# A hybrid RWKV-7 / RG-LRU layer whose engine programs are ordered by another timing model

## The chip, the cores and the metric

The kernel runs on one core of one Trainium2 chip. Times are device microseconds (us) from the first to the last instruction's work of one execution, as the run reports them; a kernel's time is the median of its runs. The core has five instruction streams that matter here: PE (matrix products, with its weight loads shown apart as PEld), DVE, ACT and POOL (element-wise work), and SP, which issues most of the DMA transfers. Each stream executes its own program strictly in the order in which it stands, and waits for the others through semaphores.

## What is computed

One layer of a diffusion backbone on 128 context tokens and 1024 latent tokens, 1024 wide. Cut to what matters:

```python
h = rmsnorm(x, ln1_g) * (1.0 + sc1) + sh1            # modulation from silu(c) @ w_mod
proj = h @ w_in                                       # r, k, v, xw, xa, xg, xb, gb
r, k, v, xw, xa, xg, xb, gb = jnp.split(proj, SPLITS, axis=-1)
ya, s_fin = rwkv7_mix(r, k, v, xw, xa, xg, s0, ...)   # 8 heads x 64, two directions
yb, h_fin = rglru_mix(xb, gb, h0, ...)                # 8 blocks x 64, two directions
x = x + g1 * (jnp.concatenate([ya, yb], axis=-1) @ w_out)
h = rmsnorm(x, ln2_g) * (1.0 + sc2) + sh2
u = dwconv(h @ w_up, ffn_conv_w, ffn_conv_b, CONV_F_LEFT, grid)
ua, ub = jnp.split(u, 2, axis=-1)
x = x + g2 * ((jax.nn.gelu(ua) * ub) @ w_down)        # then a last rmsnorm
```

`rwkv7_mix` is a recurrence over the tokens with a 64x64 state per head; the RG-LRU is a linear recurrence per channel. Outputs are the two normalised token arrays and the final context states.

## The kernel before, in words

**Precision.** Most products are made of three: an operand is split into a rounded part and a rest (`round_hi` L103, `rest_lo` L110), and `mm3` (L94) multiplies high by high, high by low and low by high. `mm` (L91) is the one place that issues a product, so that all of them carry line L92.

**Stretches.** The program goes through the following in order of time; where one ends and the next begins, they overlap.

- *Start and modulation*, to about 92 us: the inputs and a part of `w_mod` are loaded, tokens are normalised and transposed.
- *Projection*, 92 to 460 us: `proj` (L722) makes a tile of 128 columns of `h @ w_in` in three spans of 384 tokens, each a group of 24 products into one of two PSUM banks (`mm`), which ACT copies out. Beside it run, as generators that are stepped along (`beside`, L983): `unit_keys` (L539), which takes the norm of the keys through `cols2` (L474: a product into bank `uk`, an ACT copy `row`, three transposes back into `uk`, a DVE copy); `stage_ab` with `products` (L628, tile `dg`) and `bonus` (L650: two POOL operations on `kd`, then a product `ab<-kd,rkc`); and `inverse` (L488, tile `iv`), a long chain of DVE operations with a few products at its end.
- *Two lanes*, 460 to 720 us: the recurrence is worked through in hops of 64 tokens by `chain` (L1100). One hop is `prep` (L1079: product `pa<-kxa,BK`, a DVE mask `G`, a POOL scaling of `BK`, transposes, an ACT copy `Kt`) and then a serial sequence: products into `ya` with the state, copies `R` out of it, products `ca<-R,TTp`, copies `VS`, products `ca<-VS,Kt` and `ya<-VS,G`, and the addition into the next state. Lane a makes 32 hops one after the other, lane b 24. The last letter of a tile is its lane: `ya`, `ca`, `pa` are lane a's. Beside them stands the rest of the projection with the RG-LRU (`lru_gates` L863, tile `lg`; `lru_scan` L884).
- *Four lanes*, 720 to about 960 us: lanes c and d (8 hops each, tiles `yc`, `cc`, `pc` and so on) join; `post` (L1277, tile `po`) finishes outputs of the lanes; `mod_rest` (L1335, tile `md`) loads the rest of `w_mod` and multiplies; `wout_lru` (L1413, tile `wo`) makes the RG-LRU half of the output projection. Here all lanes' `p` and `c` tiles share two PSUM banks (`two`, L1442).
- *Output projection of the other half and second norm*, to about 1090 us (`second_norm` L1476); *up projection*, 1090 to 1546 us; *down projection*, 1570 to 1825 us.

**What sets the order.** The Python program emits all instructions in one sequence. Where several generators run beside each other, counts written out by hand share them out, for the two lanes and the rest of the projection, and then for the four lanes:

```python
run_all((take(lane_a, LA), LA), (take(lane_b, LB), LB), (rest_of_projection(), 12 + (54 - 6 * len(EARLY)) * 4 // PK))  # L1250
run_all((lane_a, 98 - LA), (lane_b, 98 - LB), (lane_c, 26), (lane_d, 26), (posts(90), 90),                          # L1445
        (seq(mod_rest(16, 24), beside_all((mod_rest(24, 48), 30), (wout_lru(), 48))), FL))
```

With LA = 74 and LB = 52, 24 hops of lane a and some 17 of lane b are emitted beside the projection's rest. The emitted sequence is not the engines' order yet: when the `TileContext` (L1856) is closed, a scheduler walks through it with a model of the time that each instruction takes, and puts on each engine's program the earliest emitted instruction that the model has ready. The change touches only the function `kernel` at the end, where the context is made.

## Time and profile before

| | |
|---|---|
| median of 3 runs | 1857.11 us (1849.83, 1857.11, 1857.19) |
| the profiled execution's own time | 1849.17 us |
| its span in the profile | 1847.5 us |
| PE busy, weight loads busy | 1716.4 us (93%), 1442.9 us (78%) |
| DVE, ACT, POOL busy | 1272.2, 865.5, 721.8 us |
| mean granted clock of TensorE | 0.954 of 2.4 GHz |

The profile is of one execution. Its page gives busy times by engine and by fortieth of the span; answers of the trace give the same by any stretch, the waits of an engine with what ended them, and groups of instructions with their mean duration and the idle time before them. A wait is charged to the instruction that came last. The granted clock is 1.00 where TensorE had 2.4 GHz all the time, and falls towards 0.5 with the share of time at 1.2 GHz.

### The profile page before, as it was taken

What the parts mean: (1) busy time and instruction counts of PE and PEld (TensorE: products, weight loads), DVE (VectorE), ACT (ScalarE), POOL (GpSimd) and SP (SyncE); (2) the same over time, 40 slices, a digit from 0 to 9 for tenths busy, and PEclk for the clock granted to TensorE, in tenths of its full rate; (3) what the DMA queues carried; (4) which work ended last, traced back from release to release, by engine and by line L of the source; (5) the groups of instructions that cost most, each with busy time, mean ns of one, the idle gap of its engine ahead of it and who ended that gap; (6) DMA issues with size and microseconds to landing.
All of it is one profiled execution on the core that took longest, in us unless ns stands there. A gap on an engine that the chain in (4) does not pass through costs nothing.

```text
span 1847.5 us, 35759 instructions
## 1 busy us (share of the span) xinstructions
PE 1716.4 (93%) x13341; PEld 1442.9 (78%) x13341; DVE 1272.2 (69%) x2633; ACT 865.5 (47%) x1787; POOL 721.8 (39%) x742
## 2 busy tenths in 40 slices
PE   5998898888999989899988789999999998999996
PEld 4776676678777778456656689999999998888885
DVE  5458967797477664476788877676767667576764
ACT  6466655643666756333335844444444443121211
POOL 1022423322355344131121166666666663434340
PEclk8898979889999999899999899999999999999998
DMA  9254544443443434867775222222222225558571
GB/s 300 63 163 155 174 139 135 147 147 118 145 122 97 131 104 146 257 194 231 232 254 189 82 64 86 78 72 72 74 79 75 77 73 171 184 159 262 173 252 57
DMA packets 268428, 264.92 MB, mean 143 GB/s; under 512 B 21173, under 2 KB 218448, under 8 KB 268256
## 3 DMA queue, kind: packets, MB, share of 16 engines
q1 hardware_dynamic: 252496, 245.97, 42.1%
q10 hardware_dynamic: 15472, 16.54, 2.7%
q8 instruction: 105, 1.72, 0.4%
q14 instruction: 67, 0.55, 0.1%
q0 software_dynamic: 288, 0.14, 0.0%
HBM read 188.00 MB, written 74.58 MB: 142 GB/s over the span
## 4 chain that ended last, share of the span: by engine, by line
PE 66%; DVE 9%; ACT 3%; DMA 3%; issue 3%; POOL 3%; SPq 0%; ACTq 0%; POOLq 0%; DVEq 0%
PE acc L92 14%; PE x L92 7%; PE y L92 7%; PE z L92 7%; PE mm L92 7%; PE v L92 3%; PE wo L92 3%; PE ya L92 2%; PE lg L92 2%; PE md L92 2%; PE pa L92 2%; PE ca L92 1%; DVE X L501 1%; PE yb L92 1%; DVE gt L499 1%
## 5 line engine op out<-in xcount | busy, mean ns | idle before, releaser
L92 PE MATMUL mm<-h_hi,winp 128*128 128x384 f32 x1056 | 304.4, 358 | 4.9 <-DVE vr L808 3.2
L92 PEld LDWEIGHTS mm<-h_hi,winp 128*128 128x128 f32 x1056 | 198.7, 196 | 26.4 <-issue 14.9
L92 PE MATMUL mm<-h_lo,winp 128*128 128x384 f32 x528 | 187.7, 356 | 3.0 <-DVE h_lo L112 3.0
L112 POOL TENSOR_TENSOR wl<-raw,wh 128x512 fp32r<-128x512 f32 x110 | 155.1, 1412 | 69.7 <-ACT wh L106 69.4
L106 ACT ACTIVATE wh<-raw 128x512 fp32r<-128x512 f32 x110 | 69.5, 633 | 148.3 <-PE z L92 81.0
L92 PE MATMUL x<-f_hi,wh 128*128 128x256 f32 (+1 forms) x352 | 105.8, 301 | 8.9 <-ACT q L1652 5.3
L92 PEld LDWEIGHTS mm<-h_lo,winp 128*128 128x128 f32 x528 | 103.7, 197 | 9.6 <-DVE h_lo L112 4.5
L1090 POOL TENSOR_TENSOR BK<-BK,pc 128x256 f32<-128x256 f32 x72 | 47.8, 664 | 150.5 <-PE pa L92 58.8
L92 PE MATMUL x<-f_lo,wh 128*128 128x256 f32 (+1 forms) x352 | 105.5, 300 | 0.2 <-DVE f_lo L112 0.2
L92 PE MATMUL y<-t_hi,wh 128*128 128x320 f32 (+1 forms) x352 | 104.9, 298 | 0.7 <-DVE q L1657 0.7
L92 PE MATMUL x<-f_hi,wl 128*128 128x256 f32 (+1 forms) x352 | 105.3, 299 | 0.0
L92 PE MATMUL y<-t_lo,wh 128*128 128x320 f32 (+1 forms) x352 | 104.7, 297 | 0.0
L92 PE MATMUL y<-t_hi,wl 128*128 128x320 f32 (+1 forms) x352 | 104.6, 297 | 0.0
L112 POOL TENSOR_TENSOR wl<-S,wh 128x512 fp32r<-128x512 f32 x44 | 57.7, 1311 | 105.6 <-ACT wh L106 105.6
L92 PE MATMUL acc<-f_hi 128*128 128x512 f32 x330 | 91.0, 397 | 3.2 <-ACT zf L1760 3.2
L108 POOL TENSOR_SCALAR t_hi<-raw 128x512 fp32r<-128x512 f32 x66 | 52.9, 804 | 81.6 <-PE acc L92 35.4
L1619 DVE SCALAR_TENSOR_TENSOR zf<-C,fcw,zf 128x567 f32<-128x567 f32 x66 | 63.5, 962 | 23.3 <-ACT zf L1617 23.3
L92 PEld LDWEIGHTS acc<-f_hi 128*128 128x128 f32 x330 | 63.1, 192 | 16.9 <-ACT zf L1760 3.7
L92 PEld LDWEIGHTS x<-f_hi,wh 128*128 128x128 f32 x352 | 67.9, 193 | 9.9 <-ACT q L1652 5.8
L112 DVE TENSOR_TENSOR t_hi<-raw,t_hi 128x512 fp32r<-128x512 f32 x66 | 48.1, 735 | 37.0 <-POOL t_hi L108 37.0
L1617 ACT ACTIVATE zf<-C,colB,fcw 128x576 f32<-128x576 f32 x66 | 57.3, 868 | 28.1 <-DVE C L1689 15.7
L600 POOL TENSOR_TENSOR kd<-kd,rk 128x512 f32<-128x512 f32 (+1 forms) x24 | 32.2, 1342 | 97.0 <-ACT kd L598 96.8
(516 smaller groups left out, 5211.1 us busy)
## 6 DMA issues: line engine op xcount, KB each, us to landing
raw<-in_w_down SPq DMA_DIRECT2D x132, 256.0 KB, 3.1
raw<-in_w_up SPq DMA_DIRECT2D x88, 256.0 KB, 3.0
wmod<-in_w_mod SPq DMA_DIRECT2D x68, 256.0 KB, 4.2
act_d<-zf SPq DMA_DIRECT2D x44, 288.0 KB, 2.2
src<-act_d SPq DMA_DIRECT2D x66, 192.0 KB, 3.8
win<-in_w_in SPq DMA_DIRECT2D x44, 256.0 KB, 3.9
KR<-kb_d SPq DMA_DIRECT2D x36, 256.0 KB, 3.2
VS<-v_d SPq DMA_DIRECT2D x36, 256.0 KB, 3.2
```

The costliest lines, as they stand in the source:

```text
L92: PE.matmul(out, lhsT, rhs, start=start, stop=stop, skip_group_check=True)
L106: A.activation(hi, src, AF.Copy)
L108: eng.tensor_scalar(hi, src, 1.0, 0.0, op0=OP.mult, op1=OP.add)
L112: eng.tensor_tensor(lo, src, hi.bitcast(F32), op=OP.subtract)
L499: V.tensor_tensor(tv, X[:, q + 1:32, q:q + 1].to_broadcast([128, m, q]), X[:, q:q + 1, 0:q].to_broadcast([128, m, q]), op=OP.mult)
L501: V.tensor_tensor(X[:, q + 1:32, 0:q], X[:, q + 1:32, 0:q], tv, op=OP.add)
L600: G.tensor_tensor(self.kd, self.kd, self.k, op=OP.mult)
L1090: G.tensor_tensor(bk, bk, pc_f[q.f][:, :, x:x + 1].to_broadcast([128, 2, 128]), op=OP.mult)
L1617: A.activation(u, src, AF.Identity, scale=fcw[:, 1, m:m + 1], bias=colb("ffn_conv_b", m))
L1619: V.scalar_tensor_tensor(dv[:, :, 1:64], sv[:, :, 0:63], fcw[:, 0, m:m + 1], dv[:, :, 1:64], op0=OP.mult, op1=OP.add)
```

## The change

The scheduler is told to order the engines' programs by the timing of a timeline simulator in place of a core simulator's. The emitted sequence, the tiles, the arithmetic and the DMA transfers stay.

```diff
-    with _tile.TileContext(nc) as tc:
+    with _tile.TileContext(nc, schedule_with_timeline_sim=True) as tc:
         tile_hybrid_step(tc, aps, *outs)
```

Matched by their names, all 10533 products and transposes of PE, 2633 instructions of DVE, 742 of POOL and 989 transfers of SP are the same in both programs, in another order. ACT's loads of function tables, which the build puts in where the function changes, go from 29 to 33. From the up projection to the end PE's order is the same, but for the beginning of the up projection and that of the down projection. Ahead of that it differs throughout. Three places follow; the rows are an engine's instructions in the order of its program (line, operation, output and inputs, output's shape, how often in a row).

PE in the projection, before the change: the last `dg` products of a group, and the `bonus` product `ab<-kd,rkc`, which needs two POOL operations on `kd`; `mm` is a group of the projection.

```order
L92 MATMUL dg<-kr,bk 32x32 x2
L92 MATMUL mm<-h_lo,winp 128x384
L92 MATMUL mm<-h_hi,winp 128x384 x2
L92 MATMUL mm<-h_lo,winp 128x384
L92 MATMUL mm<-h_hi,winp 128x384 x2
L92 MATMUL mm<-h_lo,winp 128x384
L92 MATMUL mm<-h_hi,winp 128x384
L92 MATMUL ab<-kd,rkc 2x512
```

The same product on PE with the change, where the `dg` rows stand 29 rows further up.

```order
L92 MATMUL mm<-h_hi,winp 128x384 x2
L92 MATMUL mm<-h_lo,winp 128x384
L92 MATMUL mm<-h_hi,winp 128x384
L92 MATMUL iv<-T_2008,off 32x32 x32
L92 MATMUL ab<-kd,rkc 2x512
```

Between the last `dg` and `ab` there were 8 products of the projection; now there are 40, and 32 of the inverse. Of the twelve such products in the program, five have moved away from `dg` like this, and seven stand closer to it than before.

PE in the projection, before: the second and third step of the key norms of one tile (`uk<-sq,hsel`, then the transposes of ACT's copy `row` of its result).

```order
L92 MATMUL mm<-h_lo,winp 128x384
L92 MATMUL uk<-sq,hsel 2x384
L92 MATMUL mm<-h_hi,winp 128x384 x2
L92 MATMUL mm<-h_lo,winp 128x384
L92 MATMUL mm<-h_hi,winp 128x384
L484 MATMUL uk<-ident,row 128x2 x3
L92 MATMUL mm<-h_hi,winp 128x384
```

The same on PE with the change.

```order
L92 MATMUL iv<-TT,a_2254 32x32 x32
L484 MATMUL uk<-ident,row 128x2 x3
L92 MATMUL uk<-sq,hsel 2x384
L484 MATMUL uk<-ident,row 128x2 x3
L92 MATMUL mm<-h_hi,winp 128x384
```

Four products of the projection stood between a product into `uk` and the transposes of its copy; now none does, in this place and in others like it.

PE near the end of the four lanes, before: a part of one round in which lanes a, c and d make a hop each.

```order
L92 MATMUL cc<-R,TTp 64x64 x4
L92 MATMUL pc<-kxc,BK 128x256 x2
L92 MATMUL cd<-R,TTp 64x64 x4
L92 MATMUL wo<-woh,ybh 128x512
L92 MATMUL wo<-wol,ybh 128x512
L92 MATMUL wo<-woh,ybl 128x512
L92 MATMUL pd<-kxd,BK 128x256 x2
L92 MATMUL wo<-woh,ybh 128x512
L92 MATMUL wo<-wol,ybh 128x512
L92 MATMUL wo<-woh,ybl 128x512
L92 MATMUL md<-wmod,silx 32x512 x4
L92 MATMUL ca<-VS,Kt 64x64 x4
```

The same part of a round with the change.

```order
L92 MATMUL cc<-R,TTp 64x64 x4
L92 MATMUL yc<-VS,G 64x64
L92 MATMUL cd<-R,TTp 64x64 x4
L92 MATMUL yc<-VS,G 64x64 x3
L92 MATMUL pc<-kxc,BK 128x256 x2
L92 MATMUL yd<-VS,G 64x64
L1094 MATMUL pa<-ident,BK 128x128 x2
L92 MATMUL yd<-VS,G 64x64 x3
L1094 MATMUL pc<-ident,BK 128x128 x2
L92 MATMUL pd<-kxd,BK 128x256 x2
L1094 MATMUL pd<-ident,BK 128x128 x2
L92 MATMUL ca<-VS,Kt 64x64 x4
```

The products of `wo` and `md` have gone from the last five rounds: the last `wo` stands ahead of lane a's 28th hop, where before it stood behind its 32nd. The projection's rest moved up likewise: its last product stands ahead of lane a's 16th hop, where before it stood just ahead of the 25th, and lane a's hops 18 to 25 now stand nearly by themselves, with products of `md`, the first of `wo`, and the first hop of lane d.

## Rows read from the trace of the kernel before

**Rows 1.** The page: the span, and the engines' busy time with its share.

```profile
span 1847.5 us, 35759 instructions
...
PE 1716.4 (93%) x13341; PEld 1442.9 (78%) x13341; DVE 1272.2 (69%) x2633; ACT 865.5 (47%) x1787; POOL 721.8 (39%) x742
```

**Rows 2.** By stretch: length, then each engine's busy time, clock, DMA share, GB/s.

```profile
92.00:460.00 368.00, 334.53 (x3677) 265.47 (x3677) 281.46 (x598) 210.43 (x475) 107.94 (x147) 0.91 0.47 147
460.00:720.00 260.00, 249.65 (x2258) 200.23 (x2257) 164.99 (x334) 173.20 (x352) 118.31 (x122) 0.97 0.39 117
720.00:800.00 80.00, 66.05 (x476) 41.74 (x476) 33.61 (x97) 32.61 (x81) 19.81 (x31) 0.90 0.65 216
800.00:930.00 130.00, 129.23 (x1058) 86.94 (x1058) 98.13 (x289) 49.00 (x139) 25.82 (x38) 1.00 0.74 236
930.00:1090.00 160.00, 131.05 (x787) 105.29 (x786) 130.58 (x298) 86.84 (x195) 44.10 (x35) 0.90 0.47 153
1090.00:1546.00 456.00, 456.00 (x3418) 455.70 (x3418) 322.71 (x555) 203.67 (x329) 293.82 (x225) 1.00 0.25 79
...
1570.00:1825.00 255.00, 255.00 (x1114) 210.84 (x1115) 160.23 (x260) 46.24 (x98) 100.21 (x120) 0.99 0.60 189
```

**Rows 3.** PE's waits, 92 to 460 us: us in total, times, longest.

```profile
PE ab L92 <- POOL kd L652: 9.0, 5, 3.1
...
PE mm L92 <- DVE vr L808: 3.2, 2, 2.2
...
PE ab L92 <- POOL P L606: 2.2, 1, 2.2
```

**Rows 4.** Groups on POOL, whole span: count, then busy us, mean ns of one.

```profile
L652 POOL TENSOR_TENSOR kd<-kd,rk 128x512 f32<-128x512 f32 (+1 forms) x12 | 15.0, 1251 | 0.7
```

**Rows 5.** PE's waits, 720 to 800 us.

```profile
PE pc L92 <- DMA BK<-kb_d: 6.8, 1, 6.8
PE pa L1094 <- DVE S0b L1185: 1.8, 1, 1.8
...
PE cc L92 <- ACT R L1075: 0.8, 1, 0.8
...
PE cc L92 <- ACT VS L1075: 0.5, 1, 0.5
PE cc L92 <- ACT Kt L1095: 0.5, 1, 0.5
```

**Rows 6.** PE's waits, 460 to 720 us.

```profile
PE ca L92 <- DVE R L1077: 5.7, 3, 4.9
```

**Rows 7.** Groups on ACT, whole span: table loads of one line.

```profile
L901 ACT ACT_TABLE_LOAD x5 | 6.4, 1283 | 0.1
```

**Rows 8.** PE in order of time: start, us, and two of lane a's hops beginning.

```profile
486.93 0.61 PE L92 MATMUL ya<-S1a,KR 128*128 128x128 f32 x4
...
493.27 0.61 PE L92 MATMUL ya<-S0a,KR 128*128 128x128 f32 x4
```

**Rows 9.** PE's waits, 800 to 930 us, all of them.

```profile
PE pc L92 <- DVE S0a L1185: 0.4, 1, 0.4
PE wo L92 <- DVE wol L112: 0.3, 1, 0.3
```

**Rows 10.** Groups on PE, 903.3 to 925.8 us, one round of hops.

```profile
L92 PE MATMUL wo<-woh,ybl 128*128 128x512 f32 x13 | 5.4, 414 | 0.0
L92 PE MATMUL wo<-woh,ybh 128*128 128x512 f32 x12 | 5.1, 429 | 0.0
L92 PE MATMUL wo<-wol,ybh 128*128 128x512 f32 x12 | 4.7, 394 | 0.0
L92 PE MATMUL md<-wmod,silx 128*32 128x512 f32 x8 | 2.1, 604 | 0.0
```

**Rows 11.** PE's waits, 930 to 1090 us.

```profile
PE mm L92 <- ACT rv L128: 4.8, 1, 4.8
PE mm L92 <- DVE tm L1408: 4.0, 5, 1.6
```

## The prediction

> **What bounds the kernel now.** I read the busy times first, then the stretches, then PE's waits in each stretch. PE is busy for 93% of the span [rows 1], but the stretches differ [rows 2]. The up projection keeps PE busy for 456.00 of 456 us and the down projection for 255.00 of 255, both at a clock of 0.99 or 1.00. PE's order there is unchanged but for the beginnings, so these 711 us can't get shorter by an order, and with their start fed as before they don't get longer. What the change can touch lies between 92 and 1090 us. PE is idle there for 368 − 334.5 = 33.5 us in the projection, 10.4 in the two lanes, 14 in the first 80 us of the four lanes, 0.8 in the next 130, and 29 up to 1090: 87.7 us in all. Two things are to be seen in the waits. Where PE waits long (2 to 7 us at a time), its program holds a product too early for an input that comes late from POOL, DVE or a DMA [rows 3, 5]. And where independent products stand between a lane's steps, PE hardly waits at all: 0.7 us in 130 [rows 9].
>
> **The change, part by part.** All instructions stay, so the work on every engine stays, apart from four more table loads on ACT. Only waits change, and the clock with them. I count in the two orders how many products stand between a product that needs a copy and the product that the copy was made from.
>
> *Projection.* `ab<-kd` waits for POOL five times, 9.0 us in all, and once more for 2.2 us [rows 3]. One POOL operation on `kd` takes 1.25 us, and two follow each other [rows 4]. In the change, five of the twelve `ab` have 7.8 to 9.6 us of products ahead of them since the last `dg`, where they had 1.7 to 5.9 us before, and four of them waited for over 2 us each. The longest wait was 3.1 us, and these five gain 3.4 to 8 us of cover, so I take 10 of these 11.2 us as gone, and the 3.2 us on `vr` too, whose cover grows likewise: −13. On the other side, the `uk` steps and others like them have lost their cover: I count 27 places in this stretch (3 before) at which less than 0.4 us of products stands between a product and one that needs ACT's or DVE's copy of its result. What such a place costs is seen at the start of the four lanes, where PE waited 0.8, 0.5 and 0.5 us for copies with nothing between [rows 5]. 27 × 0.5 = +13.5. Sum: 0, with ends of −13 (all new places hidden behind other waits) and +13.
>
> *Two lanes.* 5.7 us of waits for `R` [rows 6], most of it one wait of 4.9 us whose cover doesn't grow; I take −2 for the others, and +2 for five new uncovered places. ACT switches between exponential and square root more often, since the two square roots of an RG-LRU block no longer stand side by side: six more table loads here (and fewer elsewhere) at 1.28 us [rows 7]. ACT is busy for 173 of 260 us [rows 2], so I cost them at nothing; if ACT were in a lane's way there, it would be 6 × 1.28 = 7.7 us. Sum: 0, from −5 to +8.
>
> *Start of the four lanes.* PE waited 6.8 us for the first `BK` from DRAM, then for single handovers, 10.4 us in the five rows shown [rows 5]. With the change the projection's rest is through earlier, its memory is free earlier, and these loads run while lane a makes eight hops nearly alone. Those hops cost in turn: a hop takes 493.27 − 486.93 = 6.3 us where nothing holds it up [rows 8], so eight take 51 us. I sum the start-to-start times of the products that now stand in this piece to some 49 us. So PE has work for nearly all of it, and what is lost are handovers: 12 uncovered ones, 12 × 0.55 = +6.5, against −10.4. Sum −4, from −11 to +8; the upper end is one more late transfer of 6.8 us, since PE's program holds `md` products between lane a's steps, and a late `wmod` would hold up lane a, which is queued behind it.
>
> *End of the four lanes.* This is the term that decides. Before, a round of one hop of lanes a, c and d took 22.5 us, of which 15.2 us were products of `wo` and 3.0 or less of `md` [rows 10]; they filled every step, and the stretch ran at clock 1.00 with 0.7 us of waits [rows 2, 9]. With the change no `wo` and no `md` is left for the last five rounds, and the lanes go in step, share two PSUM banks, and wait for the same copies. I count 32 places with less than 0.4 us of cover, where there were none. At 0.55 us (between the 0.5 and 0.8 us of [rows 5]) that is +17.6. The lanes' own products in these rounds come to some 43 us; at the clock of 0.90 that the stretches with waits show, against 1.00 [rows 2], they would take 4.8 us more, of which I take half. Sum +20. It can be 0, if the three lanes cover each other as lanes a and b do around 490 us [rows 8]; at 0.8 us each it is 32 × 0.8 + 4.8 = +30.
>
> *Up to 1090 us.* The first product of the next stretch waited 4.8 us and five others 4.0 us [rows 11]. Their cover grows by 0.6 to 1 us in the change; −4, from −6 to 0. Start, up and down projection: 0. The few DMA issues that change places on SP there have PE's unbroken run in front of them; without that cover one late transfer is again 6.8 us.
>
> Sum: 0 + 0 − 4 + 20 − 4 = **+12 us** on the profiled execution's 1849.2 us. That execution is at the lower of two levels, 7.9 us under the median; the runs shown lie at 1849.8 and at 1857.1 to 1857.2. I set the 12 us on the middle of the levels, 1853, and predict **1865 us**: slower, by 0.65%. About 0.5%, or 9 us, is what a measurement of this kernel can tell from no change.
>
> **The rivals.**
>
> *Gains and losses cancel.* The lanes cover each other at the end for the larger part, and the end costs 6 us in place of 20. Then the sum is −2, and the time 1851. For it speaks the stretch around 490 us, where two lanes alone made hops at 6.3 us; against it, that there each lane had banks of its own, and the order held the lanes out of step. It decides at about 0.2 us per uncovered place.
>
> *Faster: the waits for late inputs were the real loss.* The order by the new timing puts nearly every product that waited before further behind its producer. If those longer distances hold, and the uncovered places in the projection fall into time at which PE would have waited for PSUM copies anyway, then the projection gives −13, the start of the four lanes −11, up to 1090 us −6, and the end costs 10: −20, which is 1833. For it: each wait of 2 us or more in [rows 3] but for the inverse's gets more cover. Against it: 27 places there stand bare where 3 did. The point is whether a bare place in the projection costs less than 0.2 us.
>
> *The weight loads were the bound.* In the 470 us of the lanes (460 to 930 us) PE's products are busy for 444.9 us, its weight loads for only 328.9 [rows 2]. If products that only look busy leave room, a better order can pack the lanes' small products closer, and a quarter of these 116 us would be −29: 1824. Against it: in the part with 0.7 us of waits the clock is 1.00 and DVE is at 98 of 130 us, and nothing there suggests that PE stood idle. The Trainium skill (Perfetto Trace Analysis, Identifying the Most-Contended Engine) says that the busy share of matmuls misjudges the headroom, and that the weight loads' share is the measure; by it these stretches are at 70%, not at 95%, and this rival is the forecast. The trace agrees in the up projection, where both are at 100%, and leaves it open in the lanes.
>
> That the change does nothing is excluded: the orders differ.
>
> **How the numbers follow.** The forecast, slower by over 0.5%, has a chance of 0.45; its own range, by the ends of its largest term, is 1858 to 1885. Cancelling has 0.31, the late inputs 0.19, the weight loads 0.05. So faster is 0.24, the same 0.31, slower 0.45. The range for eight times in ten leaves out the weight loads and the far ends: from 1836, a little above the second rival, to 1888, which is the upper level of 1857 with the end's +30.
>
> **What would show it.** Right: in the changed profile PE's waits for `kd` and `vr` are under 3 us together; the waits for `BK` from DRAM at the start of the four lanes are gone; the last five rounds of hops take 14 to 16 us each, at a clock under 1.00, with PE waiting for `R`, `VS`, `Kt` and `G` some 15 to 25 us in all; the up and down projections take 456 and 255 us as before. Wrong: those five rounds take 10 to 11 us each, or the projection is shorter by over 10 us or longer by as much, or PE waits for `wmod` amid lane a's hops.

## The result and the profile after

The changed kernel takes 1919.86 us (median of 4 runs, 1910.67 to 1930.05) against 1853.47 us (4 runs, 1847.04 to 1857.19): a ratio of 1.0363, 95% interval 1.0286 to 1.0441. It is slower, as forecast, but by over five times as much: 66 us where 12 were forecast, and outside the range. The changed kernel's runs lie at two levels, two near 1911 and two near 1929 us, and the profiled execution is the slowest of the four, 1930.05 us with a span of 1928.1: against the 1847.5 us of [rows 1] it is 80.6 us longer, some 14 us more than the medians differ by.

The page after: the span, and the engines' busy time.

```profile
span 1928.1 us, 35880 instructions
...
PE 1757.1 (91%) x13341; PEld 1489.1 (77%) x13341; DVE 1289.2 (67%) x2633; ACT 860.5 (45%) x1791; POOL 728.2 (38%) x742
```

DVE, ACT and POOL are as busy as in [rows 1] to within 17 us. PE is busy 41 us longer with the same products, at a mean granted clock of 0.929 where it had 0.954. By stretch, with the columns of [rows 2]; the rows after the first begin at the 2851st and the 4351st product of PE's program, and the last ends at the 5251st (the first row begins earlier than the table's projection, as in [rows 2], at 85 us):

```profile
85.00:485.30 400.30, 346.49 (x3690) 284.06 (x3689) 276.49 (x586) 207.49 (x479) 106.98 (x142) 0.85 0.42 132
485.30:823.10 337.80, 307.49 (x2386) 237.68 (x2388) 188.20 (x400) 194.41 (x382) 130.34 (x144) 0.88 0.48 151
823.10:1028.60 205.50, 188.84 (x1500) 129.85 (x1500) 132.11 (x355) 69.92 (x199) 41.91 (x59) 0.96 0.57 180
```

The same stretches of the kernel before, from product to product (the first from 92 us):

```profile
92.00:465.30 373.30, 339.44 (x3694) 268.73 (x3693) 284.35 (x602) 213.68 (x482) 109.34 (x150) 0.91 0.47 148
465.30:757.50 292.20, 272.28 (x2383) 215.37 (x2385) 175.54 (x371) 185.32 (x379) 124.81 (x132) 0.96 0.42 130
757.50:944.50 187.00, 182.25 (x1517) 120.58 (x1516) 129.59 (x376) 70.03 (x197) 39.59 (x58) 0.99 0.72 231
```

Where the 80.6 us came from, in us. "At equal work" corrects for the products that one program has done ahead of a seam and the other not yet (4.4 us at most, by their durations before). "Lost to the clock" is the stretch times what its granted clock lacks to 1.00. The first row begins with PE's first product, 2.7 us into the span; in the last one, idle time and clock are counted up to PE's last product.

| stretch | before | after | difference | at equal work | PE idle, before to after | lost to the clock |
|---|---|---|---|---|---|---|
| start, to the 451st product | 110.8 | 105.8 | −5.0 | −4.4 | 21.0 to 21.4 | 10.2 to 6.8 |
| projection | 351.8 | 376.8 | +25.0 | +26.1 | 33.9 to 51.5 | 34.1 to 59.7 |
| two lanes, lane a's solo hops with them | 292.2 | 337.8 | +45.6 | +39.5 | 19.9 to 30.3 | 11.9 to 39.3 |
| four lanes | 187.0 | 205.6 | +18.6 | +18.8 | 4.8 to 16.7 | 1.7 to 8.5 |
| up to the up projection (5860th) | 145.7 | 147.7 | +2.0 | +6.2 | 28.9 to 31.6 | 16.7 to 16.1 |
| up projection | 459.2 | 459.6 | +0.4 | +0.4 | 0 to 0 | 0.3 to 1.0 |
| down projection and end | 298.0 | 292.2 | −5.8 | −5.8 | 5.2 to 1.3 | 3.4 to 0.0 |

PE's waits in the projection after, 88 to 485 us, which answer to [rows 3]:

```profile
PE ab L484 <- ACT row L480: 10.4, 5, 4.4
PE ab L92 <- ACT b L589: 7.0, 4, 2.6
PE iv L92 <- DVE T L506: 6.7, 4, 2.9
PE dg L92 <- DVE bk L622: 4.2, 5, 1.6
PE uk L484 <- ACT row L480: 4.1, 6, 1.0
...
PE ab L92 <- POOL kd L652: 2.0, 2, 1.2
```

The waits for `kd` went from 9.0 to 2.0 us, and the one for `vr` is gone. In their place PE waits for `row` and `b` from ACT and for `T` and `bk` from DVE, small steps on both.

PE's waits in the two lanes after, 485 to 823 us, the longest ones, which answer to [rows 5, 6]:

```profile
PE ya L92 <- ACT VS L1075: 5.1, 5, 2.4
PE cb L92 <- DVE VS L1077: 4.1, 2, 3.6
PE ya L92 <- DVE S0a L1185: 3.9, 1, 3.9
PE ca L92 <- DVE VS L1077: 3.0, 2, 2.6
PE pa L92 <- DMA KR<-kb_d: 2.8, 1, 2.8
PE cb L92 <- ACT R L1075: 2.7, 2, 2.0
```

The 6.8 us for `BK` from DRAM [rows 5] are gone; one wait of 2.8 us for `KR` from DRAM is new. Otherwise the lanes' own copies and state updates are late, by 2 to 4 us at a time, on DVE as on ACT.

What ACT does in that stretch shows how copies come to be late. ACT in order of time, after:

```profile
509.76 0.27 ACT L1075 ACTIVATE R<-ya 64x128 f32<-64x128 f32 x1
510.06 1.27 ACT L1065 ACTIVATE kxa<-KR 64x512 f32<-64x512 f32 x2
511.36 1.35 ACT L896 ACTIVATE th<-th,lc 128x1152 f32<-128x1152 f32 x1
512.73 0.38 ACT L1095 ACTIVATE Kt<-pa 128x256 f32<-128x256 f32 x1
513.01 1.34 ACT L894 ACTIVATE tz<-th,lc 128x1152 f32<-128x1152 f32 x1
514.36 1.28 ACT L901 ACT_TABLE_LOAD   x1
515.66 1.16 ACT L901 ACTIVATE a<-a 128x1152 f32<-128x1152 f32 x1
516.84 1.28 ACT L896 ACT_TABLE_LOAD   x1
518.13 1.35 ACT L896 ACTIVATE th<-th,lc 128x1152 f32<-128x1152 f32 x1
519.51 1.28 ACT L901 ACT_TABLE_LOAD   x1
520.80 1.17 ACT L901 ACTIVATE a<-a 128x1152 f32<-128x1152 f32 x1
521.99 0.27 ACT L1075 ACTIVATE R<-yb 64x128 f32<-64x128 f32 x1
```

The same gate steps of the RG-LRU before, the middle of the group:

```profile
507.95 1.34 ACT L896 ACTIVATE th<-th,lc 128x1152 f32<-128x1152 f32 x1
509.41 0.27 ACT L1075 ACTIVATE VS<-cb 64x128 f32<-64x128 f32 x1
510.86 0.27 ACT L1075 ACTIVATE R<-ya 64x128 f32<-64x128 f32 x1 [1.18 <-PE ya L92]
511.03 1.34 ACT L894 ACTIVATE tz<-th,lc 128x1152 f32<-128x1152 f32 x1
512.73 0.27 ACT L1075 ACTIVATE VS<-ca 64x128 f32<-64x128 f32 x1 [0.36 <-PE ca L92]
512.91 1.34 ACT L896 ACTIVATE th<-th,lc 128x1152 f32<-128x1152 f32 x1
```

Before, copies `R` and `VS` of the lanes stand between the gate steps shown. After, no `R` and no `VS` runs on ACT from 510.0 to 522.0 us, while five gate steps and three table loads go through nearly in one piece; the last product into `yb` ends at 516.5 us, so the `R<-yb` at 521.99 starts 5.5 us late. There are four such groups in the stretch. Added up over the records of the two lanes, from the moment a copy's input and its target were free to its start, the copies `R` and `VS` on ACT (88 before, 82 after between these seams) wait 69 us instead of 31, and the `Kt` 34 instead of 17. DVE hangs on the same copies. `R` and `VS` are each made in two halves, one by ACT and one by DVE, and in all 82 pairs of either trace DVE's half starts only after ACT's has ended. DVE's waits for that, 485 to 823 us after:

```profile
DVE VS L1077 <- ACT VS L1075: 32.6, 22, 3.9
DVE R L1077 <- ACT R L1075: 20.3, 18, 4.0
```

These 52.9 us were 21.5 before. So a wait that is put down to DVE's half can go back to ACT's. And in the chain of waits (the work that ended last, followed back), the pieces on ACT between 485 and 823 us add up to 56 us; between 465 and 757 us before they were 17. Those on PE are 216 and 212. That is what the experiments start from.

### The profile page after: what moved, and what is told of

Its sections match the earlier page's. It is cut to its first block, busy times and chain, and to the rows that moved or that the text cites. A ratio compares the mean times of both kernels' runs of the same rounds, so it can differ in the third digit from the quotient of the medians.

```text
span 1928.1 us, 35880 instructions
## 1 busy us (share of the span) xinstructions
PE 1757.1 (91%) x13341; PEld 1489.1 (77%) x13341; DVE 1289.2 (67%) x2633; ACT 860.5 (45%) x1791; POOL 728.2 (38%) x742
## 4 chain that ended last, share of the span: by engine, by line
PE 64%; DVE 7%; ACT 6%; DMA 3%; issue 3%; POOL 2%; SPq 1%; ACTq 0%; DVEq 0%; POOLq 0%
PE acc L92 14%; PE mm L92 8%; PE x L92 7%; PE y L92 7%; PE z L92 7%; PE v L92 3%; PE ya L92 2%; PE wo L92 2%; PE lg L92 2%; PE md L92 2%; PE pa L92 2%; PE yb L92 1%; PE ca L92 1%; PE pb L92 1%; ACT xt L1486 1%
## 5 line engine op out<-in xcount | busy, mean ns | idle before, releaser
L92 PEld LDWEIGHTS mm<-h_hi,winp 128*128 128x128 f32 x1056 | 206.5, 203 | 17.6 <-issue 6.8
L112 POOL TENSOR_TENSOR wl<-raw,wh 128x512 fp32r<-128x512 f32 x110 | 149.6, 1361 | 134.8 <-ACT wh L106 134.8
L92 PEld LDWEIGHTS mm<-h_lo,winp 128*128 128x128 f32 x528 | 107.6, 204 | 8.7 <-issue 4.0
L92 PE MATMUL x<-f_lo,wh 128*128 128x256 f32 (+1 forms) x352 | 105.8, 301 | 0.5 <-DVE f_lo L112 0.5
L92 PE MATMUL y<-t_hi,wh 128*128 128x256 f32 (+1 forms) x352 | 104.6, 297 | 0.0
L92 PE MATMUL y<-t_lo,wh 128*128 128x256 f32 (+1 forms) x352 | 104.5, 297 | 0.0
L92 PE MATMUL y<-t_hi,wl 128*128 128x256 f32 (+1 forms) x352 | 104.2, 296 | 0.0
L92 PEld LDWEIGHTS x<-f_lo,wh 128*128 128x128 f32 x352 | 68.2, 194 | 0.8 <-DVE f_lo L112 0.8
L92 PEld LDWEIGHTS x<-f_hi,wl 128*128 128x128 f32 x352 | 68.2, 194 | 0.0
```

The source lines that it names most:

```text
L92: PE.matmul(out, lhsT, rhs, start=start, stop=stop, skip_group_check=True)
L112: eng.tensor_tensor(lo, src, hi.bitcast(F32), op=OP.subtract)
```

## The experiments

Most of these kernels hold engines to a written order. Each instruction gets an edge to its predecessor in a list, which the scheduler has to keep; the rest of the kernel stays.

```diff
     with _tile.TileContext(nc, ...) as tc:
         tile_hybrid_step(tc, aps, *outs)
+        _pin(nc, tc, {'PE': (0, 99999), 'DVE': (0, 99999), ...})

+            if prev is not None:
+                tc.add_manual_dep(have[f"I-{n}"], prev, info, reason="order")
+            prev = f"I-{n}"
```

**Is it the order, and whose?** `t_all` keeps the changed timing, and holds all five engines to the order of before; `t_pe` holds PE alone.

> The change stays in (timeline timing), but every engine's order is held to that of the kernel before. If the loss comes from the order alone, this is the kernel before again: 1853 us, within 0.5%. If something else of the change costs time (other buffers, other semaphores, more waits), it stays above that, up to 1920 us.

> The change stays in, and TensorE alone is held to its order of before; VectorE, ScalarE, GpSimd and the queues are ordered by the timeline timing around it. Theory 1, that TensorE's own order makes the loss (more matmuls placed right behind what they read, so more waits, so a lower granted clock): about 1855 us, with the granted clock of the two lanes (465 to 720 us) back at about 0.97. Theory 2, that the order on the other engines makes it (copies for TensorE that stand behind large vector operations): about 1900 to 1920 us.

> The reverse of the run beside it: the timing of before, with TensorE alone held to the change's order. Theory 1 (TensorE's own order): about 1905 to 1920 us, with a clock of about 0.88 in the two lanes. Theory 2 (the other engines' order): about 1855 us. If both orders have to come together, both this run and the one beside it stand well below 1920 us.

`t_all` took 1852.75 us, ratio 1.0012 (0.9993 to 1.0031): the change acts through the order, and through nothing else to within 0.3%. `t_pe` took 1923.52 us, 1.0385 (1.0357 to 1.0412), and `e3_core_pe` 1980.11 us, 1.0699 (1.0672 to 1.0725). So theory 1 and theory 2 both fell: before's order of PE, with the other engines ordered anew around it, is as slow as the change, and the change's order of PE with others is slower than either. (In either run the engines left free have an order of their own, neither before's nor the change's, so neither run tests a half of the change's order as it stands.) In `t_pe` the loss begins in the first 110 us (+12.6) and goes through all stretches up to the up projection. The third expectation, that both runs stand well below 1920 us, fell as well: half of an order kept costs the whole loss or more. The five orders belong together.

**In which stretch?** `e4_proj` holds all engines to before's order up to 465 us; `m_a485` has the change's exact order up to 485 us, then before's.

> The change stays in, with all five engines held to the order of before only up to the end of the input projection (TensorE's first 2851 instructions, 465 us before); the lanes and the feed-forward part are free. The traces of before and of the change differ by 20 us at that place. If the stretches add up: 1920 less 20, about 1900 us. If the loss of the lanes is only the end of a chain that began in the projection, nearly all goes: about 1860 us. If the lanes lose more when the projection leaves them other work: 1910 us or more.

> The change's exact order on all five engines for everything that it had started by 485 us (end of the input projection in its trace), and the order of before for all that is left. If the stretches lose independently: 1853 plus the 20 us that the change is late at that place, about 1873 us. If the loss of the lanes is prepared in the projection: 1890 to 1920 us. If before's lanes win time back from work done early: about 1860 us.

`e4_proj`: 1891.81 us, 1.0217 (1.0187 to 1.0246). `m_a485`: 1886.50 us, 1.0182 (1.0138 to 1.0227). So 25 to 35 us belong to the projection's order, 10 of the 35 lost at the seam (the 2851st product comes at 495.7 us, where the change has it at 485.3), and 30 to 40 to the order from the lanes on. In `m_a485` the two lanes take 300.6 us, 37 less than with the change's order from the same start, so the lanes' loss is not prepared in the projection. (`e4_proj` was 10 us late at its seam as well.)

**Is it the clock behind the waits?** 27 us of the two lanes' loss and 26 of the projection's stand beside a lower clock. `e8_warm_after` (the change) and `b_warm` (before) put matmuls of no use ahead of 14 and 12 waiting ones. Their exact order stays; the results are overwritten.

```diff
         tile = ps_pool.tile([128, 512], F32, name=name, tag=f"b{i}", bufs=1)
+        _fill(PE, ident, tile, name)
...
+        [PE.matmul(tile[:, 0:w], ident, ident[:, 0:1].to_broadcast([128, w]), ...) for _ in range(n)]
```

> The change's exact order, with matmuls of no use (identity times a column of it, 128x256, into the PSUM tile that the waiting matmul overwrites) put right ahead of 14 of the matmuls that wait 1.3 us or more between 88 and 1110 us. No wait is made shorter; TensorE is only kept busy in it. Theory 'clock' (the larger part of the loss is the granted clock that falls behind long waits; 125 us times the missing share are lost so between 90 and 1200 us, 65 in before): 20 to 40 us faster than the change, about 1885 to 1900 us, with a mean granted clock above the 0.929 of the change. Theory 'waits' (the clock costs little, or falls for another reason): no gain, 1915 to 1925 us.

> The same for the kernel before, in its exact order: matmuls of no use ahead of 12 of the matmuls that wait 1.3 us or more. Theory 'clock': 15 to 35 us faster than before, about 1820 to 1838 us, granted clock above 0.954. Theory 'waits': 1853 us, or a few us more.

The change with them took 1922.74 us, 1.0358 (1.0305 to 1.0411); before with them 1850.61 us, 0.9988 (0.9967 to 1.0008). In before the clock rose: 0.961 to 0.972 in its ten runs, 0.942 to 0.961 in the 19 of before beside them. In the change it is 0.937 to 0.945 in four runs, against 0.929 to 0.943, so `b_warm` tells more. The time fell in neither. One 6.8 us wait [rows 5] shows how (PE in order of time, in `b_warm`; its `mm` is L94, and the 15 matmuls of no use are 30 records):

```profile
737.48 0.27 PE L999 MATMUL lg<-ident,lru_fin 128*8 128x128 f32 x1
737.58 6.70 PE L1872 MATMUL pc<-ident 128*128 128x256 f32 x30
744.59 0.67 PE L94 MATMUL pc<-kxc,BK 128*128 128x256 f32 x2 [0.31 <-DMA BK<-kb_d]
```

By stretch, `b_warm`, against the first two rows of before above:

```profile
93.00:467.00 374.00, 351.29 (x3764) 280.41 (x3763) 284.21 (x602) 213.68 (x482) 110.51 (x150) 0.92 0.47 148
467.00:758.30 291.30, 279.68 (x2421) 221.96 (x2423) 175.91 (x371) 185.09 (x379) 125.33 (x132) 0.97 0.42 130
```

PE is busy for 19 us more and at a higher clock, and both stretches are as long as before. 24.7 us of its time are the matmuls of no use. The others take 5.5 us less, and the waits, filled or not, 5.3 us more: in before, what the clock gave back PE spent waiting. In the change the two lanes lost 23 us to the clock instead of 39, their useful products took 10 us less, half of it came back as waits, and the stretch became 5 us shorter, which one trace can't tell from none (see the square roots below). So theory "clock" fell as far as it was tested. That is not all of it: `b_warm` gave back 8.5 of the 46 us that these two stretches lose to the clock in before, and `e8_warm_after` 8 of the 60 us that the change's projection loses, with a projection of 375.8 us instead of 376.8 (a wait whose PSUM tile was still being read could not be filled).

**And where PE is waited for?** `e7_stall` puts stalls into the up projection of before, with PE's order held there:

```diff
+            if c == 1 and (2 <= m < 9 or 12 <= m < 19 and j in (1, 4)):
+                hi = w[0].rearrange("p k c -> p (k c)")
+                for part in [hi[:, 0:512:384]] if m < 9 else [hi] * 4:
+                    A.activation(part, part.bitcast(F32), AF.Copy)
```

> The kernel before, with stalls put into the up projection, where TensorE has no wait and the granted clock is 1.00 (one unit of the projection takes 20.8 us there): between two matmul groups ScalarE copies part of the weights that both read onto itself. In units 2 to 8 seven short stalls each (2 columns), in units 12 to 18 two long ones each (four copies of 512 columns). If a stall costs what it lasts: seven short ones of about 0.7 us add 5 us to a unit, two long ones of about 3 us add 6 us, and the clock stays at 1.00. If long waits draw the clock down and that is paid in a stretch that TensorE bounds: units 12 to 18 take 4 to 10 us more than the stalls last, at a clock of 0.75 to 0.9, and units 2 to 8 not.

The kernel took 1939.68 us, 1.0470 (1.0423 to 1.0517). One unit with seven short stalls, one with none (22.4 us, as in before; the 20.8 of the expectation was wrong), one with two long ones:

```profile
1161.90:1187.70 25.80, 24.16 (x170) 22.32 (x169) 14.51 (x28) 11.01 (x23) 14.49 (x11) 1.00 0.21 65
1313.30:1335.70 22.40, 22.40 (x170) 22.40 (x169) 15.85 (x29) 9.98 (x16) 14.58 (x11) 1.00 0.24 74
1420.40:1451.10 30.70, 25.33 (x169) 24.81 (x169) 15.71 (x28) 14.91 (x24) 14.55 (x11) 0.89 0.18 55
```

PE's waits in the last of them:

```profile
PE y L92 <- ACT wh L1729: 2.8, 1, 2.8
PE z L92 <- ACT wh L1729: 2.6, 1, 2.6
```

A short stall costs (25.8 − 22.4) / 7 = 0.49 us, while the profile shows 1.64 / 7 = 0.23 us of idle time for it. A long one costs (30.7 − 22.4) / 2 = 4.2 us for 2.7 us of wait, since each is followed by products at 1.2 GHz: 11% of 30.7 us, 1.7 us a stall. None of the 49 short stalls lowered the clock, and all 14 long ones did. So a wait of 2.7 us is paid one and a half times where PE sets the pace. What `b_warm` took off the clock where PE has waits of its own was worth nothing.

**Can ready work fill the waits?** `b_fill` pulls the next ready matmuls ahead of waiting ones in before, at 15 places (17 in the expectation), the first of them:

```diff
 L92 MATMUL mm<-h_lo,winp 128x384
-L92 MATMUL mm<-h_hi,winp 128x384
+L92 MATMUL mm<-h_hi,winp 128x384 x2
+L92 MATMUL mm<-h_lo,winp 128x384
 L92 MATMUL ab<-kd,rkc 2x512
-L92 MATMUL mm<-h_hi,winp 128x384
-L92 MATMUL mm<-h_lo,winp 128x384
```

> The order of before on all engines, but ahead of 17 matmuls that wait, TensorE gets the next matmuls of its program whose operands and PSUM bank were free by then in the trace (25 us of 77 us of waits of 0.5 us and more are covered so). If waits cost what they last: about 1828 us. If the clock behind them comes on top: about 1810 to 1820 us. If the waits only move to later matmuls, whose cover is used up: 1845 to 1855 us.

1853.73 us, 1.0010 (0.9982 to 1.0038): nothing. PE's idle time between 90 and 1200 us fell from 87.5 to 82.6 us, not by 25. The stretch ahead of the up projection became 7.4 us shorter, and the up projection 9.3 us longer, with 5.9 us of waits that it did not have. So the waits came again at later products.

**Is it lane steps that stand behind others?** Lane steps that were ready in the change's trace and had to wait in their engine's queue are put ahead: on ACT and DVE, on PE, on all three; and in `e16_chain` on PE in the projection too, but only those that waited over 1.5 us.

The rule by which the orders were made, in short:

```diff
-    key[n] = start[n]
+    key[n] = min(start[n], ready[n])        # lane steps; sorted by key, the rest keeps its place
```

> The change's exact order, but between 485 and 825 us each of the lanes' own steps on ScalarE and VectorE (copies out of PSUM, masks, state updates; 481 instructions) stands ahead of the gate and recurrence steps that in the trace of the change started after it was ready and before it ran. In that trace these steps wait 136 us on ScalarE (89 in before) and 137 us on VectorE (144). Theory 'copies' (the hops are slow because ScalarE's copies stand behind its 1.2 to 1.4 us gate steps; lane a's first 16 hops take 254 us against 153): the two-lane stretch gets 20 to 35 us shorter, 1885 to 1900 us in all. Theory 'matmuls' (the hops are slow because TensorE's program has projection groups ahead of them): below 8 us, 1912 to 1920 us.

> The change's exact order, but between 485 and 825 us each matmul and transpose of the lanes stands on TensorE ahead of the projection and gate matmuls that started after it was ready. Theory 'matmuls': the two-lane stretch gets 20 to 35 us shorter, 1885 to 1900 us in all. Theory 'copies': below 8 us, 1912 to 1920 us. If what holds the stretch is neither (the sum of TensorE's work and of what its waits and the fall of its clock take has to be placed somewhere), the waits move to the projection's own matmuls and neither run gains.

> Both edits at once, in the same stretch. If the lanes' pace is what is lost, on whichever engine: as fast there as before, 30 to 45 us gained, 1875 to 1890 us. If the two edits only move the waits to the projection's groups, 1905 to 1920 us.

> The change's exact order, but on TensorE between 106 and 825 us a product of the serial chains (dg, ab, iv, uk, pv of the projection; y, c and p tiles of the lanes) that was ready for over 1.5 us stands ahead of the products that started after that (206 of 2380 waited so long). Theory 'fillers first' (the change places projection products as soon as they are ready, so that chain products wait 384 us there against 223 in before): the projection 10 to 20 us shorter, 1900 to 1910 us. Theory 'spread', and what the lanes showed when their matmuls went first without that margin: no gain, 1915 to 1960 us.

| run | time, us | ratio (95%) | two lanes, us (change: 337.8) |
|---|---|---|---|
| `e9_copies` | 1923.64 | 1.0389 (1.0357 to 1.0421) | 334.3 |
| `e10_matmuls` | 1966.51 | 1.0626 (1.0571 to 1.0681) | 377.4 |
| `e11_both` | 1986.39 | 1.0720 (1.0684 to 1.0756) | 402.4 |
| `e16_chain` | 1946.45 | 1.0495 (1.0461 to 1.0529) | 352.9 |

None gains, and three lose 15 to 65 us in the two lanes; the projection of `e16_chain` takes 381.4 us instead of 376.8. In `e9_copies` ACT's pieces of the chain between 485 and 819 us fell from 56 to 35 us, as meant, but those on DMA rose from 17 to 31, on POOL from 9 to 16, on DVE from 20 to 27, and DVE's halves still waited 51 us for ACT's. PE's longest waits there:

```profile
PE ya L92 <- DVE S1a L1185: 5.0, 3, 2.2
PE ya L92 <- DVE S0a L1185: 4.4, 1, 4.4
PE pa L1094 <- DVE G L1087: 4.0, 2, 3.8
```

Two of these three are not in the change's own list above, and the third, `S0a`, has grown. So a late copy that is put right makes the next one late. Why the matmuls put ahead lose so much was not looked into; the trace shows only that the last RG-LRU product comes at 792 us in place of 765.

**One exact piece.** In each of the four gate groups the change has the first square root between the two exponentials. `e13_sqrt` takes that out of the change; `e14_sqrt_before` puts it alone into before.

```diff
-  L894 L896 L894 L901 L896 L901     (ACT, lane copies between them left out)
+  L894 L896 L894 L896 L901 L901
```

> The change's exact order, but ScalarE's first square root of each of the four groups of gate steps stands behind the last exponential, next to the second square root, as in before. That takes out 8 of 33 table loads (1.283 us each, 10.3 us of ScalarE). Theory 'gate steps' (what ScalarE does in one piece there is on the chain that sets the two lanes): 8 to 15 us faster than the change, 1905 to 1912 us, all of it between 485 and 823 us. Theory 'spread' (no single engine's steps set the stretch; a wait taken away turns up elsewhere): within 5 us of the change, 1915 to 1925 us.

> The reverse: before's exact order, but in the four groups of gate steps the first square root stands ahead of the last exponential, as the change has it: 35 table loads instead of 29, 7.7 us more of ScalarE between 465 and 757 us. Theory 'gate steps': 6 to 12 us slower than before, 1859 to 1865 us. Theory 'spread': before's lanes have the slack, 1853 us within 4.

Table loads on ACT over the whole span, `e13_sqrt`:

```profile
L901 ACT ACT_TABLE_LOAD x4 | 5.1, 1283 | 0.1
```

And in `e14_sqrt_before`, which has as many at these two lines as the change, against the five of [rows 7] and none at L896 before:

```profile
L901 ACT ACT_TABLE_LOAD x8 | 10.3, 1283 | 0.1
L896 ACT ACT_TABLE_LOAD x4 | 5.1, 1283 | 0.1
```

`e14_sqrt_before` took 1860.21 us against 1852.43, ratio 1.0032 (1.0013 to 1.0051): 2.4 to 9.4 us for six more loads, 7.7 us of ACT. The two lanes became 7.0 us longer than in before's row above:

```profile
467.10:766.30 299.20, 275.81 (x2383) 216.84 (x2385) 175.43 (x371) 192.73 (x385) 122.49 (x132) 0.95 0.40 125
```

That is more than before's order varies there: it took 292.2 us, 293.4 in `t_all` and 292.4 in `e7_stall`. So ACT's gate steps are on the chain even in before, where ACT is busy for 185 of 292 us, and the piece costs before some 7 us. In the change itself its worth is not shown. `e13_sqrt` took 1917.27 us, 1.0359 (1.0319 to 1.0399), which tells nothing from the change's own 1.0363. In its trace the two lanes are 331.1 us, 6.7 less, but the five traces that have the change's order up to 485 us (the change, `e9_copies`, `e10_matmuls`, `e11_both`, `e13_sqrt`) differ by 10 us in the projection, 371.0 to 381.1, so one trace can't tell 6.7 us. What the two runs do show is that ACT's place in the chain was no measure of the loss: taking the eight loads out brings ACT's pieces in the two lanes from 56 to 20 us, putting six in brings them from 17 to 42, and the stretch moves by 7 us or less. A load takes 1283 ns. The Trainium skill (ScalarE: Activation LUTs, What ACT_TABLE_LOAD costs) gives about 1283 ns, and the trace agrees.

**The counts that share out the emission.** In the change both lanes go in step, and lane a's last eight hops of this part stand alone from 770 to 823 us.

```diff
-LA = 74
+LA = 50
```

> The change with LA = 50 instead of 74: of lane a 16 hops instead of 24 are emitted beside the projection's rest, so that both lanes end there together and the other 8 hops come among the four lanes' work. If the solo stretch (770 to 823 us, 8 hops) is part of the loss: 10 to 30 us faster than the change, 1890 to 1910 us. If those hops cost as much among the four lanes: 1915 to 1925 us; if the last rounds get longer for it, up to 1950 us.

> The change with LA = 62, 20 hops of lane a beside the projection's rest. If the solo stretch is part of the loss, about half of what LA = 50 gains; if not, as LA = 50: 1915 to 1930 us.

1913.25 us, 1.0312 (1.0284 to 1.0341), and 1917.50 us, 1.0336 (1.0306 to 1.0366). With LA = 50 no hop of lane a stands alone any more, and by the ratios some 9 of the 66 us are won back, which the intervals don't tell from none. The solo stretch is not the loss, or only a small part of it.

**The best of both.** `best` has the change's order for what it had started by 100 us and for what before had not started by 1480 us, and before's between.

> Before's order, except that what the change had started by 100 us stands in the change's order at the front, and what before had not started by 1480 us stands in the change's order at the end (the down projection and the output). By the traces the start is 5 us shorter in the change and the down projection 7 us. If both keep: 1841 us, 0.6% under before. If the seam at 100 us costs what the seam at 485 us did (10 us): 1850 us or more.

1852.11 us, 0.9985 (0.9965 to 1.0004): no gain to be told. In its trace 2.0 us of the start's gain are left at the 451st product, and the projection behind the seam is 7 us longer. No run here beats before.

## Why the prediction was wrong in size

**What it had right.** The direction. The waits for `kd` and `vr` are under 3 us together, the one for `BK` at the start of the four lanes is gone, and up and down projection keep their pace. The end of the four lanes, "the term that decides", was put at +20 (0 to +30); the stretch lost 18.6 us, and in the last five rounds PE is idle for 82.00 − 67.00 = 15.0 us:

```profile
960.00:1042.00 82.00, 67.00 (x695) 48.82 (x694) 63.48 (x203) 34.87 (x109) 17.53 (x26) 0.92 0.30 86
```

Its parts fit less well, so the closeness of the sum is partly luck. The rounds between lane a's last five hops take 21.7, 21.3, 17.7 and 16.2 us, where 14 to 16 were forecast; PE is busy for 67 us where the lanes' own products were put at 43 (lane b's last hop and `po` run there too, and the clock is 0.92); and PE's waits for `VS`, `Kt` and `G` make 7.8 us of the "15 to 25", beside 2.7 for POOL's `BK`. The price of a place without cover, 0.5 to 0.55 us, is of the size of the 0.49 us that a short stall costs in `e7_stall`, but of those only 0.23 show as idle time, and the forecast priced idle time.

**What failed: "Two lanes. Sum: 0".** With the start of the four lanes it was −4; it measured +39.5 at equal work. The step behind it was to "count in the two orders how many products stand between a product that needs a copy and the product that the copy was made from". That is cover on PE alone, and it does not set the time: `t_pe` has PE's order as before, every place covered as before, and is 71 us slower. How long the copy itself stands on ACT or DVE was not counted, and there the change's trace shows gate steps and table loads in one piece and lane copies behind them. The order of ACT was open to be read, as PE's was. The same paragraph had the right mechanism and dropped it: "ACT is busy for 173 of 260 us, so I cost them at nothing; if ACT were in a lane's way there, it would be 6 × 1.28 = 7.7 us." `e14_sqrt_before` puts six loads into before, and measures 7.8 us (2.4 to 9.4). A busy share of 67% says nothing on whether a copy of 0.27 us stands behind one operation or behind eight.

**What failed: "Projection. Sum: 0, from −13 to +13".** It measured +26. The −13 came true nearly in full (12.2 us of waits for `kd` and `vr` became 2.0). The other side was priced at 27 × 0.5, but there stand waits of 2 to 4 us for `row`, `b` and `T`, steps that are late, not bare handovers. A projection longer by over 10 us was the prediction's own sign of being wrong. That the same step failed here is argued from these waits; no run moved those copies alone. And the sum has no term for the clock, to which the projection lost 25.6 us more and the two lanes 27.4; what part of that is a price stays open.

**What failed in the range.** Both stretches were bounded by their counts of uncovered places, and no bound allowed for the engines that feed PE. The prediction's "own range, by the ends of its largest term", 1858 to 1885, does not follow from its sum either: with 0 and +30 for the end of the four lanes that gives 1845 to 1875.

**The smaller terms.** Up to 1090 us: −4 forecast, +2.0 measured, +6.2 at equal work. Start and down projection: 0 forecast, −5.0 and −5.8 measured; less is lost to the clock in both (3.4 us each), and 3.9 us less to waits in the down projection.

**The rivals.** Cancelling and the late inputs fell with the sign. The third, that weight loads were the bound, is not borne out: with the order changed they fill 238/338 = 70% of the two lanes, where it was 215/292 = 74%, and the stretch became longer.

**What stays open.** That the order makes the loss is shown; which part of the order makes it is not, for the larger part. The split square roots cost some 7 us in before; neither they nor the filled waits gave the change back anything that could be told from its spread. For the rest of the two lanes' 39.5 us, and for the projection's 26, no single edit gave anything back: not the copies first, not the matmuls first, not the counts. That late copies on ACT lie on the chain is seen in the trace; that they are the cause is argued, not shown, for where they were put ahead other steps became late. Left to try are the halves of `R` and `VS` made on one engine, so that DVE no longer waits for ACT, and a whole order made for measured times.

## What to carry to other kernels

An order is one thing over all engines: before costing a reordering by the cover on the busiest engine, read on every engine that feeds it what now stands ahead of its small copies. A wait that a busy engine shows is a price only where that engine sets the pace; keep it busy through the wait, and see whether the stretch gets shorter, before its idle time or its clock is counted as loss. An engine's share of the chain that ended last is a clue and not a price: here it went from 56 to 20 us and the time did not follow. Hold the old order with edges to get a control that tells a scheduler's order from everything else that a flag may change.

## What the runs showed of the hardware

Two things had not been expected. PE's granted clock can be raised without any gain: 80 matmuls of no use in 12 waits took it from 0.954 to 0.966 in the profiled executions, and the time stayed the same to within 0.4%. And stalls of 2.6 to 2.9 us all drew the clock to 1.2 GHz for a while, 1.7 us of loss each, where seven stalls in 26 us, 1.64 us of idle time in all, never did. The Trainium skill (Perfetto Trace Analysis, Optimization Strategy) advises to find the gaps on the most contended engine and what blocks it there; here PE, busy for 93% of the span, had its gaps filled in two ways, with ready work and with useless work, and neither trace agrees that this is where time is to be won. That section goes on to make the blocking work start sooner; the run here that did so, `e9_copies`, won nothing either (1.0389 against the change's 1.0363).
